# Scores from a high part over a low part, h's place per sublayer, and other distances between softmax stages, in a four-layer trunk

## The chip, the cores and the metric

The kernel runs on one core of one Trainium2 chip. The metric is the device time of one launch in microseconds (us), lower is better. The core has TensorE (PE, matmuls and transposes), VectorE (DVE), ScalarE (ACT), GpSimd (POOL) and SyncE (SP, which issues the loads here); each works through its own list of instructions in order.

## What is computed

Four layers over 512 tokens of width 1024, each a token mixer and a SwiGLU channel mixer (ffn), with a modulation from `c` ahead of each and a layer norm behind it. The change touches the scores of layer 1 (sliding-window attention, swa) and layer 3 (differential attention, diff), h's place in memory in all eight sublayers, and one yield in layer 0 (mLSTM). Cut to these:

```python
for i in range(DEPTH):
    mod = einsum('bd,sde->sbe', silu(c), ada_w[i]) + ada_b[i]          # "ada": 24 columns a sublayer
    h = x * (1 + scale[0]) + shift[0]
    y = (mlstm, swa, hgrn2, diff)[i](h)
    x = layer_norm(alpha * x + (1 + gate[0]) * y)
    h = x * (1 + scale[1]) + shift[1]
    y = swiglu(h, ffn_w_in[i], ffn_w_out[i])
    x = layer_norm(alpha * x + (1 + gate[1]) * y)

# swa: 16 query heads of 64, 2 key heads; 128-query blocks, 256 keys (128 in the first)
s = where(valid, einsum('bqhgd,bkhd->bhgqk', qi, ki) * scale, -inf)
mx = maximum(s.max(-1), sink); p = exp(s - mx); p = p / (p.sum(-1) + exp(sink - mx))

# diff: 8 heads, two score maps each, q and k of 64; 128-query blocks, all keys up to the block's end
p = softmax(where(causal, einsum('bqhcd,bkhcd->bhcqk', qi, k) * scale, -inf))
a = p[:, :, 0] - lam * p[:, :, 1];  out = einsum('bhqk,bkhe->bqhe', a, v)
```

## The kernel before

**Products.** A float32 product is made of fp32r matmuls: `weights` loads a 128 x 1024 tile into one of seven `raw` buffers, ACT rounds it to `wh` (L194), DVE subtracts to get `wl` (L195), and `mm3` issues high x high, high x low and low x high (L204 to L206). h is kept split as well, `hh` and `hl`, one tile each for the whole kernel. The ffn's first half works with seven products of quarters of its operands (`strassen`, L503): some of these take a quarter of h as it is, others a sum of quarters, which is in a tile `tf`. In swa and diff the scores were a single float32 matmul: q of two heads, transposed, lies in the 128 partitions, and the key side `kz` has one head's rows and zeros in the other's, so that one stationary q serves both heads.

**Swa.** A unit is a pair of heads j and a block of 128 queries tb; 8 x 4 units. `unit` is a generator with three stages: scores with mask and maximum (L943, L946 on DVE), exponentials on ACT (L953), DVE's sums, POOL's scaling (L959); then the transposes of the probabilities (L965) and their copy (L967); then the product with v (L974). `pipeline(us, (0, 5, 6))` runs stage 2 five units behind stage 1, and stage 3 six behind. The first half, j = 0 to 3, is merged with the second half's projection of q, which ends with flipping q (transposes, L924); the second half, j = 4 to 7, is merged with half of the output projection. The rotation of q and k (`rope`) is DVE and ACT work on a projection's PSUM bank.

**Diff.** Four groups g of two heads j. A unit is one j and one block tb: two scores of tb + 1 times 128 keys (L1086), mask and maximum (L1088, DVE), exponentials (L1094, ACT), reciprocal and scaling (L1097 and L1098 DVE, L1099 POOL), the combination of both maps (L1100, DVE); then the transposes (L1106) and a copy; then the product with v (L1114); then norm and flip of the output. `flip` (L1038) transposes q or k of one j. `proj(g + 1)`, which makes the next group's q, k and v, is merged with `attend(g)` as fill; for the last group half of the output projection is.

**What sets the order.** `merge` takes in turn the generator that is furthest behind, by the cost that its yields have named against its total. That gives a program order. A scheduler then lists each engine's instructions by its own estimate of when operands and buffers are there; what comes first in the program has priority. PSUM is eight banks of 128 x 512 (`bank()`), taken in turn by all of this; `b4` and `b2` are tiles of pools in SBUF. On the chip each engine keeps its list's order, and PE waits where an operand is late.

**ada.** `weights` also calls `ada_steps`: columns of the next modulations (a load into `raw` and a DVE operation, L128) are spread over the program. `fold` (L341, DVE) adds a finished output tile to the residual.

## Time and profile before

| | us |
|---|---|
| median of 3 runs (2433.79 to 2435.41) | 2435.06 |
| the profiled execution: its own time / its span | 2436.47 / 2434.8 |
| mLSTM, 0 to 238 | 238 |
| swa, 605 to 770 | 165 |
| hgrn, 1135 to 1440 | 305 |
| diff, 1808 to 2058 | 250 |
| the four ffn: from 238, 770, 1440, 2058 | 367, 365, 368, 377 |

In the rows that follow, a group's row gives line, engine, operation, output and inputs, count, then busy time in us, mean ns of one, and the idle time of the engine ahead of them with what ended it. A row of a window gives its length, each engine's busy time with the count of instructions, then the granted TensorE clock (1.00 is full), the share of DMA time and GB/s. A row of the timeline gives start, length and instruction; of the chain that ended last, start, length and line; of the waits, who waited for whom, us in total, times and the longest. A matmul's length runs until its result is there, so matmuls overlap; what one costs is the distance of their starts. A float32 matmul is two records.

### The profile page before, as it was taken

What the parts mean: (1) busy time and instruction counts of PE and PEld (TensorE: products, weight loads), DVE (VectorE), ACT (ScalarE), POOL (GpSimd) and SP (SyncE); (2) the same over time, 40 slices, a digit from 0 to 9 for tenths busy, and PEclk for the clock granted to TensorE, in tenths of its full rate; (3) what the DMA queues carried; (4) which work ended last, traced back from release to release, by engine and by line L of the source; (5) the groups of instructions that cost most, each with busy time, mean ns of one, the idle gap of its engine ahead of it and who ended that gap; (6) DMA issues with size and microseconds to landing.
All of it is one profiled execution on the core that took longest, in us unless ns stands there. A gap on an engine that the chain in (4) does not pass through costs nothing.

```text
span 2434.8 us, 40054 instructions
## 1 busy us (share of the span) xinstructions
PE 2378.1 (98%) x15464; PEld 2123.0 (87%) x15464; DVE 1794.9 (74%) x3137; ACT 1102.6 (45%) x1917; POOL 481.8 (20%) x734
## 2 busy tenths in 40 slices
PE   7999999999899999999999999999999999999998
PEld 5778999998668989899888899898988888999897
DVE  6956988886887978787755569788867556968565
ACT  2534644343553635244333336352445554635343
POOL 5003200004434000006433331000053223100003
PEclk9999999999999999999999999999999999999999
DMA  9832363743411363652521113637525111333331
GB/s 317 285 118 87 105 216 95 245 142 121 144 53 53 103 209 114 232 188 85 162 79 61 35 57 117 205 107 236 186 94 173 62 36 44 109 112 101 106 102 35
DMA packets 93999, 312.31 MB, mean 128 GB/s; under 512 B 10736, under 2 KB 13168, under 8 KB 93808
## 3 DMA queue, kind: packets, MB, share of 16 engines
q1 hardware_dynamic: 92800, 309.43, 39.6%
q8 instruction: 121, 1.98, 0.3%
q14 instruction: 70, 0.57, 0.1%
q10 hardware_dynamic: 1008, 0.32, 0.1%
HBM read 307.62 MB, written 2.10 MB: 127 GB/s over the span
## 4 chain that ended last, share of the span: by engine, by line
PE 80%; DVE 9%; ACT 4%; DMA 3%; POOL 3%; issue 2%; POOLq 0%; ACTq 0%; DVEq 0%; SPq 0%
PE ps L503 27%; PE ps L204 14%; PE ps L206 14%; PE ps L205 14%; DVE wl L195 2%; PE ps L1086 1%; DMA raw<-in_ada_w 1%; PE ps L1252 1%; DVE raw L128 1%; ACT wh L194 1%; PE ps L943 1%; DVE xz L412 1%; POOL H L448 1%; DVE xz L420 1%; DVE hl L449 1%
## 5 line engine op out<-in xcount | busy, mean ns | idle before, releaser
L194 ACT ACTIVATE wh<-raw 128x1024 fp32r<-128x1024 f32 (+1 forms) x251 | 257.9, 1031 | 382.9 <-DMA raw<-in_ffn_out 116.1
L480 ACT ACTIVATE wh<-raw 128x1024 fp32r<-128x1024 f32 x252 | 266.1, 1060 | 351.2 <-PE ps L503 134.2
L503 PE MATMUL ps<-tf,wh 128*128 128x256 f32 x2304 | 410.8, 280 | 0.0
L195 DVE TENSOR_TENSOR wl<-raw,wh 128x1024 fp32r<-128x1024 f32 (+1 forms) x251 | 304.3, 1214 | 99.8 <-ACT wh L194 84.2
L481 DVE TENSOR_TENSOR wl<-raw,wh 128x1024 fp32r<-128x1024 f32 x252 | 305.9, 1221 | 80.1 <-ACT wh L480 78.3
L503 PEld LDWEIGHTS ps<-tf,wh 128*128 128x128 f32 x2304 | 353.3, 188 | 0.9
L503 PE MATMUL ps<-tf,wl 128*128 128x256 f32 x1152 | 321.7, 279 | 0.0
L205 PE MATMUL ps<-pair,wh 128*128 128x512 f32 (+1 forms) x816 | 294.4, 361 | 1.5 <-DVE pair L578 1.3
L204 PE MATMUL ps<-pair,wh 128*128 128x512 f32 (+1 forms) x816 | 294.9, 361 | 0.0
L206 PE MATMUL ps<-pair,wl 128*128 128x512 f32 (+1 forms) x816 | 293.9, 360 | 0.0
L128 DVE CUSTOM_DVE_ANT_0 raw<-raw,cond,adab 128x1024 f32<-128x1024 f32 x192 | 246.6, 1294 | 45.3 <-DMA raw<-in_ada_w 43.9
L341 DVE SCALAR_TENSOR_TENSOR xz<-ps,gate,xz 128x512 f32<-128x512 f32 (+1 forms) x208 | 129.8, 625 | 159.7 <-PE ps L206 159.3
L503 PE MATMUL ps<-hh,wl 128*128 128x256 f32 x864 | 245.0, 284 | 0.0
L503 PE MATMUL ps<-hh,wh 128*128 128x256 f32 x864 | 244.7, 283 | 0.0
L503 PE MATMUL ps<-hl,wh 128*128 128x256 f32 x864 | 244.6, 283 | 0.0
L204 PE MATMUL ps<-wh,hh 128*128 128x512 f32 (+1 forms) x608 | 239.3, 395 | 4.6 <-ACT hh L445 3.3
L204 PE MATMUL ps<-hh,wh 128*128 128x256 f32 (+1 forms) x616 | 208.0, 344 | 18.1 <-ACT wh L194 15.6
L206 PE MATMUL ps<-wh,hl 128*128 128x512 f32 (+1 forms) x608 | 222.5, 366 | 0.0
L205 PE MATMUL ps<-wl,hh 128*128 128x512 f32 (+1 forms) x608 | 222.3, 366 | 0.1
L503 PEld LDWEIGHTS ps<-tf,wl 128*128 128x128 f32 x1152 | 216.7, 188 | 0.0
L206 PE MATMUL ps<-hh,wl 128*128 128x256 f32 (+1 forms) x616 | 209.9, 343 | 5.5 <-DVE wl L195 5.5
L205 PE MATMUL ps<-hl,wh 128*128 128x256 f32 (+1 forms) x616 | 207.9, 340 | 0.2
(292 smaller groups left out, 4957.9 us busy)
## 6 DMA issues: line engine op xcount, KB each, us to landing
raw<-in_ada_w SPq DMA_DIRECT2D x192, 512.0 KB, 4.6
raw<-in_ffn_dp SPq DMA_DIRECT2D x144, 512.0 KB, 3.9
raw<-in_ffn_out SPq DMA_DIRECT2D x64, 448.0 KB, 3.6
raw<-in_ffn_in SPq DMA_DIRECT2D x32, 512.0 KB, 3.7
raw<-in_ffn_out SPq DMA_DIRECT2D x32, 512.0 KB, 4.6
raw<-in_m_vo SPq DMA_DIRECT2D x16, 512.0 KB, 5.8
raw<-in_h_qf SPq DMA_DIRECT2D x16, 512.0 KB, 4.1
raw<-in_h_ig SPq DMA_DIRECT2D x16, 512.0 KB, 3.8
```

The source lines that it names most:

```text
L128: self.nc.vector.tensor_tensor_reduce(w, w, self.cond, 1.0, self.adab[:, sub, j : j + 1], ALU.mult, ALU.add, mod[:, j : j + 1])
L194: nc.scalar.activation(hi[:, :n], raw[:, :n], AF.Copy)
L195: (eng or nc.vector).tensor_tensor(lo[:, :n], raw[:, :n], hi[:, :n].bitcast(F32), ALU.subtract)
L204: nc.tensor.matmul(ps, lhs[0], rhs[0], start=start, stop=False)
L205: nc.tensor.matmul(ps, lhs[0], rhs[1], start=False, stop=False)
L206: nc.tensor.matmul(ps, lhs[1], rhs[0], start=False, stop=stop)
L341: nc.vector.scalar_tensor_tensor(z, ps[:, t], gate[:, d : d + 1], z, ALU.mult, ALU.add)
L412: V.tensor_tensor(z, z, st[:, 0, :], ALU.subtract)
L420: V.tensor_tensor(z, z, st[:, 1, :], ALU.mult)
L480: nc.scalar.activation(hi, raw, AF.Copy)
L481: nc.vector.tensor_tensor(lo, raw, hi.bitcast(F32), ALU.subtract)
L503: nc.tensor.matmul(ps[:, j * 256 : j * 256 + 256], w[a][:, c], m[b], start=first and j == k == a == b == 0, stop=k == 3 and a == 1, skip_g ...
```

## The change

- **h's place.** `hh` and `hl` get tiles that are 128 elements longer. `place(ffn)` lets h begin 16 elements (64 bytes) further in them for an ffn than for a mixer. Pools change places and sizes (`state` behind `sm`; `mod` 24 columns for 32; `lns` 2 for 38), so everything behind them shifts.
- **Scores.** `stacked` makes, for each head of a pair, a tile with the high part of its 64 rows of q in one half of the partitions and their low part in the other. `doubled` makes k's high part, and its low part, in both halves. `mm4` issues q against high and against low: with both halves stacked, two fp32r matmuls give all four partial products. A matmul is at least 256 wide. Zeros and their memsets go. Evictions are now halves of 64 partitions: per pair of heads two on ACT and two on DVE for q, four and four for k.
- **Waiting q and k.** Rotated q (swa) and q and k (diff, in `qkdone` alike) wait in `raw` buffers, two token tiles to a buffer, and not in `b2`. `big` has 13 buffers (12), `mid` 9 (10).
- **Distances.** swa (0, 5, 7) for (0, 5, 6), diff (0, 3, 5, 8) for (0, 3, 4, 6).
- **Diff's flips.** `turn` flips q and k of one j. j = 0's stays in `proj`; j = 1's now opens the group's loop, with three steps of the units after each half, ahead of the merge.
- **mLSTM.** A yield of 2.0 for 0.0 ahead of the transposes of the output, and 11.5 for 9.5 as the total of `mix`.

```diff
-        self.state = pool("state", 1)
         self.adap = pool("adap", 2)
         self.lnp = pool("lnp", 1)
         self.sm = pool("sm", 2)
+        self.state = pool("state", 1)
...
-            self.big, self.mid = pool("big", 12), pool("mid", 10)
+            self.big, self.mid = pool("big", 13), pool("mid", 9)
...
-        self.hh = self.state.tile([P, KD, T], F32R, name="hh")
-        self.hl = self.state.tile([P, KD, T], F32R, name="hl")
+        self.hboth = [self.state.tile([P, KD * T + P], F32R, name=x) for x in ("hh", "hl")]
+        self.place(False)
...
+    def place(self, ffn):
+        o = 16 if ffn else 0
+        self.hh, self.hl = (x[:, o : o + KD * T].rearrange("p (k t) -> p k t", t=T) for x in self.hboth)
...
-        mod = self.adap.tile([P, 32], F32, tag="mod", name=self.nm("mod"), bufs=3)
+        mod = self.adap.tile([P, 24], F32, tag="mod", name=self.nm("mod"), bufs=3)
...
+    def stacked(self, ps):
+        x = self.b4([P, 2, T], F32R)
+        for h in range(2):
+            r, o = slice(64 * h, 64 * h + 64), slice(64 - 64 * h, 128 - 64 * h)
+            self.nc.scalar.activation(x[r, h, :], ps[r, :], AF.Copy)
+            self.nc.vector.tensor_tensor(x[o, h, :], ps[r, :], x[r, h, :].bitcast(F32), ALU.subtract)
+        return x
+    def doubled(self, ps):
+        hi, lo = (self.b4([P, 2, T], F32R) for _ in range(2))
+        for h in range(2):
+            r, o = slice(64 * h, 64 * h + 64), slice(64 - 64 * h, 128 - 64 * h)
+            for x in (r, o):
+                self.nc.scalar.activation(hi[x, h, :], ps[r, :], AF.Copy)
+            for x in (r, o):
+                self.nc.vector.tensor_tensor(lo[x, h, :], ps[r, :], hi[r, h, :].bitcast(F32), ALU.subtract)
+        return hi, lo
+    def in_pairs(self, xs, tt):
+        if tt % 2 == 0:
+            x = self.raw.tile([P, 2, T], F32, tag="raw", name=self.nm("raw"))
+            xs += [x[:, 0, :], x[:, 1, :]]
+        return xs[tt % 2 - 2]
+    def mm4(self, ps, q, ks):
+        for i, k in enumerate(ks):
+            self.nc.tensor.matmul(ps, q, k, start=i == 0, stop=i == 1)
...
-            self.lnp.tile([P, w], F32, tag=x, name=self.nm(x), bufs=2)[:, :2] for x, w in (("lns", 38), ("lnv", 2))
+            self.lnp.tile([P, w], F32, tag=x, name=self.nm(x), bufs=2)[:, :2] for x, w in (("lns", 2), ("lnv", 2))
...
-            yield 0.0
+            yield 2.0
             yield from self.transpose_out(y, 2, acts)
...
-            yield from self.merge((mix(h), 9.5), (fill, 26 if h == H - 2 else 20.8))
+            yield from self.merge((mix(h), 11.5), (fill, 26 if h == H - 2 else 20.8))
...
-            q = self.b2([P, T])
-            self.rope(q, ps, tt, 8)
-            qts.append(q)
+            self.rope(self.in_pairs(qts, tt), ps, tt, 8)
...
-            for jj in range(2):
-                qT = self.b4([P, 2, T])
-                for j in (2 * jj, 2 * jj + 1):
-                    ps = self.bank()
-                    for tt in range(NTT):
-                        nc.tensor.transpose(
-                            ps[:, tt * P : (tt + 1) * P], qt[tt][:, j * P : (j + 1) * P], self.ident
-                        )
-                    nc.scalar.activation(qT[:, j % 2, :], ps, AF.Copy)
-                    qTs.append(qT[:, j % 2, :])
-                    yield 0.5
+            for j in range(4):
+                ps = self.bank()
+                for tt in range(NTT):
+                    nc.tensor.transpose(ps[:, tt * P : (tt + 1) * P], qt[tt][:, j * P : (j + 1) * P], self.ident)
+                qTs.append(self.stacked(ps))
+                yield 0.5
...
-            ps = self.bank()[:, : 2 * nk * P].rearrange("p (h k) -> p h k", h=2)
-            nc.tensor.matmul(ps, qTs[j][:, q], kz[:, :, k0 : k0 + nk * P], start=True, stop=True)
+            ps = self.bank().rearrange("p (h k) -> p h k", h=2)
+            for h in range(2):
+                self.mm4(ps[:, h, :], qTs[j][:, h, q], [x[:, h, k0 : k0 + 2 * P] for x in ks])
...
-            yield from self.pipeline(us, (0, 5, 6))
+            yield from self.pipeline(us, (0, 5, 7))
...
-        for h in range(2):
-            r = slice(64 * h, 64 * h + 64)
-            nc.scalar.activation(kz[r, h, :], ps[r, :], AF.Copy)
+        ks = self.doubled(ps)
...
-            qT = self.b4([P, 2, T])
-            kz = []
-            for j in range(2):
-                if j:
-                    for _ in range(4):
-                        yield next(pv)
-                nc.scalar.activation(qT[:, j, :], flip(qk, j), AF.Copy)
-                z = self.b4([P, 2, T])
-                nc.gpsimd.memset(z[64:, 0, :], 0.0)
-                nc.gpsimd.memset(z[:64, 1, :], 0.0)
-                ps = flip(qk, 2 + j)
-                for m in range(2):
-                    r = slice(64 * m, 64 * m + 64)
-                    nc.scalar.activation(z[r, m, :], ps[r, :], AF.Copy)
-                kz.append(z)
-                yield 1.0
+            yield from turn(g, 0, qk)
             yield from pv
-            res[g] = qT, kz, v
+            res[g] = qk, v
+        def turn(g, j, qk):
+            q = self.stacked(flip(qk, j))
+            yield 0.5
+            res[g, j] = q, self.doubled(flip(qk, 2 + j))
+            yield 0.5
 
         def unit(g, j, tb, hd):
-            qT, kz, v = res[g]
+            qT, ks = res[g, j]
+            v = res[g][1]
             w = (tb + 1) * P
             q = slice(tb * P, w)
             mx, su = (self.small([P, 2], t, bufs=4) for t in ("mx", "su"))
             pr = []
             for m in range(2):
                 ps = self.bank()
-                nc.tensor.matmul(ps[:, :w], qT[:, j, q], kz[j][:, m, :w], start=True, stop=True)
+                n = max(w, 256)
+                self.mm4(ps[:, :n], qT[:, m, q], [x[:, m, :n] for x in ks])
...
-            yield from self.pipeline(us, (0, 3, 4, 6))
+            yield from self.pipeline(us, (0, 3, 5, 8))
 
         yield from proj(0)
         for g in range(4):
             fill = proj(g + 1) if g < 3 else self.out_proj(self.out_srcs(a["d_out"], 0), 2, acts[:4], gate, False)
-            yield from self.merge((attend(g), 17), (fill, 33 if g < 3 else 20.8))
+            units = attend(g)
+            for _ in turn(g, 1, res[g][0]):
+                for _ in range(3):
+                    yield next(units)
+            yield from self.merge((units, 17), (fill, 32 if g < 3 else 20.8))
...
+            self.place(more and plan[i + 1][0] == "ffn")
```

The lines of the changed kernel stand further down: `mm3` is L210 to L212, `mm4` L248, `stacked` subtracts in L226, `doubled` in L236, the flips are L954 (swa) and L1064 (diff), swa's transposes L993, diff's L1124.

**First place: the start of diff's first group, PE.** In the order's rows a name with a number is one tile (`ps_18188` one use of a PSUM bank); `wh_18205,hh` and the like are fill, the next group's projection. Before, from unit 0's scores:

```order
L1086 MATMUL ps_18188<-b_2563_18106,b_2561_18099 128x128
L1086 MATMUL ps_18192<-b_2563_18106,b_2561_18099 128x128
L204 MATMUL ps_18233<-wh_18205,hh 128x512
L205 MATMUL ps_18233<-wl_18206,hh 128x512
L206 MATMUL ps_18233<-wh_18205,hl 128x512
L204 MATMUL ps_18234<-wh_18205,hh 128x512
L205 MATMUL ps_18234<-wl_18206,hh 128x512
L206 MATMUL ps_18234<-wh_18205,hl 128x512
L1086 MATMUL ps_18243<-b_2563_18106,b_2561_18099 128x256
L1086 MATMUL ps_18247<-b_2563_18106,b_2561_18099 128x256
L204 MATMUL ps_18233<-wh_18205,hh 128x512
L205 MATMUL ps_18233<-wl_18206,hh 128x512
```

Now, from the last score of unit 1; `ps_18302` and `ps_18369` hold the flipped q and k of j = 1, and the first L1124 is unit 0's transpose:

```order
L248 MATMUL ps_18338<-b_2563_18238,b_2561_18228 128x256
L248 MATMUL ps_18338<-b_2564_18239,b_2561_18228 128x256
L248 MATMUL ps_18352<-b_2563_18238,b_2561_18228 128x384
L248 MATMUL ps_18352<-b_2564_18239,b_2561_18228 128x384
L248 MATMUL ps_18357<-b_2563_18238,b_2561_18228 128x384
L248 MATMUL ps_18357<-b_2564_18239,b_2561_18228 128x384
L1064 MATMUL ps_18369<-ident,raw_18076 128x128 x2
L1064 MATMUL ps_18369<-ident,raw_18143 128x128 x2
L1124 MATMUL ps_18384<-ident,b_2572_18317 128x128
L248 MATMUL ps_18390<-b_2563_18238,b_2561_18228 128x512
L248 MATMUL ps_18390<-b_2564_18239,b_2561_18228 128x512
L248 MATMUL ps_18395<-b_2563_18238,b_2561_18228 128x512
```

The six fill matmuls between one unit's scores and the next's are gone from here, the flips of j = 1 have come, and unit 0's transpose, which came behind 24 fill matmuls, comes right behind the second flip.

**The same place on DVE.** L1088 is mask and maximum, L1100 the combination that ends a unit's probabilities. Before:

```order
L1088 ISA b_2575_18194,mx_18186<-ps_18192,difmask 128x128
L1088 ISA mx_18186 128x1
L1092 TENSOR_SCALAR mx_18186<-mx_18186 128x2
L195 TENSOR_TENSOR wl_18541<-raw_18538,wh_18540 128x1024
L1097 RECIPROCAL su_18187<-su_18187 128x2
L1088 ISA b_2595_18245,mx_18241<-ps_18243,difmask 128x256
L1088 ISA mx_18241 128x1
L1098 TENSOR_TENSOR su_18187<-su_18187,coef 128x2
L1088 ISA b_2597_18249,mx_18241<-ps_18247,difmask 128x256
L1088 ISA mx_18241 128x1
L1100 SCALAR_TENSOR_TENSOR b_2573_18190<-b_2575_18194,su_18187,b_2573_18190 128x128
L1092 TENSOR_SCALAR mx_18241<-mx_18241 128x2
```

Now (L1106 is mask and maximum, L226 and L236 the low parts of q and k, L1118 the combination of unit 0):

```order
L226 TENSOR_TENSOR b_2568_18307<-ps_18302,b_2568_18307 64x512
L1106 ISA b_2580_18341,mx_18331<-ps_18338,difmask 128x256
L1106 ISA mx_18331 128x1
L1106 ISA b_2584_18355,mx_18350<-ps_18352,difmask 128x384
L1106 ISA mx_18350 128x1
L1115 RECIPROCAL su_18313<-su_18313 128x2
L1110 TENSOR_SCALAR mx_18331<-mx_18331 128x2
L1106 ISA b_2586_18360,mx_18350<-ps_18357,difmask 128x384
L1106 ISA mx_18350 128x1
L1116 TENSOR_TENSOR su_18313<-su_18313,coef 128x2
L236 TENSOR_TENSOR b_2589_18375<-ps_18369,b_2588_18374 64x512
L1118 SCALAR_TENSOR_TENSOR b_2572_18317<-b_2574_18322,su_18313,b_2572_18317 128x128
```

Ahead of unit 0's combination stood one unit's maxima and one weight tile; now stand the maxima of two units more, both low parts of q and one of k's.

**Second place: the middle of swa, PE.** Before, with the scores of units 17 to 19 and unit 16's transposes (L965):

```order
L204 MATMUL ps_6790<-b_1012_6755,wh_6783 128x512
L205 MATMUL ps_6790<-b_1012_6755,wh_6783 128x512
L206 MATMUL ps_6790<-b_1012_6755,wl_6784 128x512
L943 MATMUL ps_6807<-b_829_5848,b_1005_6720 128x512
L943 MATMUL ps_6824<-b_829_5848,b_1005_6720 128x512
L943 MATMUL ps_6841<-b_829_5848,b_1005_6720 128x512
L943 MATMUL ps_6858<-b_829_5848,b_1005_6720 128x256
L965 MATMUL ps_6872<-ident,b_1018_6769 128x128 x2
L943 MATMUL ps_6880<-b_829_5848,b_1005_6720 128x512
```

Now, with unit 16's transposes in L993:

```order
L248 MATMUL ps_6928<-b_861_6132,b_1005_6789 128x256
L211 MATMUL ps_6871<-b_1012_6829,wh_6864 128x512
L212 MATMUL ps_6871<-b_1012_6829,wl_6865 128x512
L248 MATMUL ps_6928<-b_862_6133,b_1005_6789 128x256
L248 MATMUL ps_6948<-b_861_6132,b_1009_6806 128x256
L248 MATMUL ps_6948<-b_862_6133,b_1009_6806 128x256
L248 MATMUL ps_6948<-b_861_6132,b_1009_6806 128x256
L248 MATMUL ps_6948<-b_862_6133,b_1009_6806 128x256
L993 MATMUL ps_6965<-ident,b_1019_6850 128x128 x2
L248 MATMUL ps_6973<-b_861_6132,b_1009_6806 128x256
```

Twelve fill matmuls stood between unit 16's scores (ahead of them) and unit 17's, and the scores were float32; now fp32r scores of five units, with a few fill matmuls among them, are all that lies between.

**The same place on DVE.** Before (L946 is mask and maximum):

```order
L967 COPY b_1009_6742<-ps_6737 128x512
L195 TENSOR_TENSOR wl_7397<-raw_7394,wh_7396 128x1024
L946 ISA b_1018_6769,mx_6764<-ps_6767,swamask,sink 128x128
L946 ISA mx_6764 128x1
L946 ISA b_1018_6769,mx_6764<-ps_6767,swamask,sink 128x128
L946 ISA mx_6764 128x1
L211 TENSOR_TENSOR b_1012_6755<-ps_6681,b_1012_6755 128x512
L949 TENSOR_TENSOR es_6765<-sink,mx_6764 128x2
L950 TENSOR_SCALAR mx_6764<-mx_6764 128x2
```

Now (L974 is mask and maximum, `b_1019_6850` unit 16's tile):

```order
L226 TENSOR_TENSOR b_1005_6789<-ps_6784,b_1005_6789 64x512
L226 TENSOR_TENSOR b_1009_6806<-ps_6801,b_1009_6806 64x512
L226 TENSOR_TENSOR b_1011_6820<-ps_6815,b_1011_6820 64x512
L226 TENSOR_TENSOR b_1005_6789<-ps_6784,b_1005_6789 64x512
L226 TENSOR_TENSOR b_1009_6806<-ps_6801,b_1009_6806 64x512
L226 TENSOR_TENSOR b_1011_6820<-ps_6815,b_1011_6820 64x512
L217 TENSOR_TENSOR b_1012_6829<-ps_6753,b_1012_6829 128x512
L226 TENSOR_TENSOR b_1014_6837<-ps_6832,b_1014_6837 64x512
L974 ISA b_1019_6850,mx_6842<-ps_6845,swamask,sink 128x128
L974 ISA mx_6842 128x1
L974 ISA b_1019_6850,mx_6842<-ps_6845,swamask,sink 128x128
L974 ISA mx_6842 128x1
```

Ahead of unit 16's maxima stood a weight tile; now also stand seven halves of the second half's q.

More of the change, by code (lines that the diff above doesn't have):

```diff
@@ L817, in mlstm @@
             fill = proj(h + 1)
-            yield from self.merge((mix(h), 9.5), (fill, 26 if h == H - 2 else 20.8))
+            yield from self.merge((mix(h), 11.5), (fill, 26 if h == H - 2 else 20.8))
         yield from self.merge(
-            (mix(H - 1), 9.5), (self.out_proj(self.out_srcs(a["m_out"], 0), 2, acts[:4], gate, False), 20.8)
+            (mix(H - 1), 11.5), (self.out_proj(self.out_srcs(a["m_out"], 0), 2, acts[:4], gate, False), 20.8)
         )
@@ L900, in swa @@
         nc.scalar.dma_start(sink, a["s_sink"].partition_broadcast(P))
-        kz = self.b4([P, 2, T])
         gp = nc.gpsimd
-        gp.memset(kz, 0.0)
         kv_ = self.b4([P, 2, NTT, P])
@@ L946, in unit @@
                 nc.vector.tensor_tensor_reduce(
-                    s[:, h, :], ps[:, h, :], ms, 0.125, sk[:, h : h + 1], ALU.add, ALU.max, mx[:, h : h + 1]
+                    s[:, h, :], ps[:, h, : nk * P], ms, 0.125, sk[:, h : h + 1], ALU.add, ALU.max, mx[:, h : h + 1]
                 )
@@ L1043, in qkdone @@
         def qkdone(tt, ps):
-            x = self.b2([P, T])
-            self.rope(x, ps, tt, 8)
-            qks.append(x)
+            self.rope(self.in_pairs(qks, tt), ps, tt, 8)
         def proj(g):
```

## The prediction

> **What bounds the kernel now.** I read the page's engine totals first, then the chain that ended last, then the windows of the stages that the change touches.
>
> ```profile
> PE 2378.1 (98%) x15464; PEld 2123.0 (87%) x15464; DVE 1794.9 (74%) x3137; ACT 1102.6 (45%) x1917; POOL 481.8 (20%) x734
> PE 80%; DVE 9%; ACT 4%; DMA 3%; POOL 3%; issue 2%; POOLq 0%; ACTq 0%; DVEq 0%; SPq 0%
> 605.00:770.00 165.00, 157.99 (x969) 117.99 (x968) 128.00 (x446) 85.31 (x240) 67.66 (x127) 1.00 0.25 82
> 647.00:751.00 104.00, 101.99 (x595) 68.58 (x593) 82.85 (x335) 54.91 (x185) 37.55 (x79) 1.00 0.15 48
> 770.00:1135.00 365.00, 361.74 (x2527) 337.50 (x2526) 302.06 (x419) 169.59 (x222) 51.27 (x85) 1.00 0.48 154
> 1808.00:2058.00 250.00, 245.21 (x1459) 208.09 (x1459) 156.03 (x480) 135.14 (x346) 69.60 (x124) 1.00 0.26 83
> 1843.00:2040.00 197.00, 194.55 (x1123) 163.04 (x1122) 117.03 (x390) 106.24 (x297) 42.59 (x81) 1.00 0.23 73
> ```
>
> TensorE is busy 98% of the span. The windows are the swa layer and its attention part, one ffn, the diff layer and its attention part (columns: length, then PE, weight loads, DVE, ACT, POOL). Even in attention PE stands still for only 2.0 us (104.00 − 101.99) in swa and 2.5 us in diff. So a matmul made shorter is worth its time, if its operands come as early as PE then wants them; DVE has room on average (20% free in swa's attention, 40% in diff's), which says nothing of single places. The profiled execution took 2436.47 us, 1.7 more than its span and 1.4 more than the median of the runs, 2435.06; I sum against 2436.5 and take 1.4 off at the end. A measurement of this kernel can tell about 0.2% (4.9 us) from no change.
>
> **Scores as two fp32r products.** One f32 score matmul is two records in the trace.
>
> ```profile
> L943 PE MATMUL ps<-b,b x64: 377/592/602, 647.2 to 738.4; 128*128 128x512 f32 x48, 128*128 128x256 f32 x16
> 640.07 0.12 PE ps L205
> 650.32 0.23 PE ps L206
> 650.55 0.88 PE ps L943 x2
> L1086 PE MATMUL ps<-b,b x128: 270/434/595, 1843.7 to 2027.8; 128*128 128x128 f32 x32, 128*128 128x256 f32 x32, 128*128 128x384 f32 x32, 128*128 128x512 f32 x32
> 1843.69 0.61 PE L1086 MATMUL ps<-b,b 128*128 128x128 f32 x4
> 1845.52 1.03 PE L1086 MATMUL ps<-b,b 128*128 128x256 f32 x4
> 1847.77 0.81 PE L1086 MATMUL ps<-b,b 128*128 128x384 f32 x2
> ```
>
> In the chain of waits each piece is the time from one matmul to the next: 0.12 us for a 256-wide fp32r matmul, 0.23 for a 512-wide one, 0.88 for a 512-wide f32 score (both records). In swa 24 such scores and 8 of half the width cost 24 × 0.87 + 8 × 0.43 = 24.3 us; after, every unit has four 256-wide fp32r matmuls, 32 × 4 × 0.12 = 15.4 us: **−8.9 us**. In diff a record takes (0.61 − 0.27)/3 = 0.11 us at 128 (0.27 is the least duration of that line), about 0.22, 0.32 and 0.43 at the other widths, so the four units of one j, two maps of two records each, cost 4 × 1.08 = 4.3 us. After: widths 256, 256, 384, 512, two maps of two products, 4 × (0.12 + 0.12 + 0.17 + 0.23) = 2.6 us (0.17 interpolated). 1.75 us × 8 = **−14 us**. This presumes that PE finds its operands, which is the question of the next two parts.
>
> **The wait at each start of a diff group.** Before, unit 0's scores went in between fill matmuls, and its transposes came long after its softmax.
>
> ```profile
> 1844.56 0.29 DVE L1088 CUSTOM_DVE_ANT_0 b<-ps,difmask 128x128 f32<-128x128 f32 x1
> 1844.77 0.28 DVE L1088 CUSTOM_DVE_ANT_0 b<-ps,difmask 128x128 f32<-128x128 f32 x1
> 1847.53 0.35 DVE L1100 SCALAR_TENSOR_TENSOR b<-b,su,b 128x128 f32<-128x128 f32 x1 [0.24 <-POOL b L1099]
> 1851.83 0.27 PE L1106 MATMUL ps<-ident,b 128*128 128x128 f32 x1
> L1088 DVE CUSTOM_DVE_ANT_0 b<-ps,difmask 128x384 f32<-128x384 f32 x16 | 8.5, 550 | 1.3 <-PE ps L1086 1.3
> 667.89 0.60 DVE b L211
> ```
>
> Scores start at 1843.69, the probabilities are ready at 1847.88 (1847.53 + 0.35), the transpose runs at 1851.83: 4 us of cover. The order of the changed kernel has taken that cover away. With j = 1's `turn` at the group's start, PE does four transposes of q, twelve score matmuls of units 0 to 2, four transposes of k, and then wants unit 0's transpose; six score banks and two flip banks are all eight of PSUM, so no fill can stand there. That is 8 × 0.11 + 4 × (0.12 + 0.12 + 0.17) = 2.5 us of PE work. Unit 0's first score is out after about 0.9 us (0.45 of transposes, two products, 0.2 until the result is there). From then DVE has, in its order, two mask-and-max of 128 (0.21 each by their starts), two q subtractions (0.60 each, the L211 row; 64 rows of 512 are not in this trace, and I take the same), two of 256 (0.34), two of 384 (0.48), five small operations (0.1), one k subtraction (0.60), and unit 0's combine (0.35): 4.7 us. The transpose can start at 0.9 + 4.7 = 5.6, PE is there at 2.5: **a wait of 3.1 us**. Unit 1's transposes wait about 0.3 us more (a subtraction, three small ones and a 0.40 combine, 1.3 us, against four 512-wide products, 0.9), and the second halves of k some 0.5 us. Some 4 us a group, four groups: **+16 us** (from 0, if DVE works through its queue sooner than this count has it, to 22, if ACT's exponentials and POOL's step come on top of it). Diff's scores thus net +2 us, between −14 and +8.
>
> **The wait in the middle of swa.** After four heads' pairs the second half of q is flipped.
>
> ```profile
> 697.24 1.36 PE L924 MATMUL ps<-ident,b 128*128 128x128 f32 x11
> 705.47 0.38 PE L965 MATMUL ps<-ident,b 128*128 128x128 f32 x2
> 697.44 0.69 DVE L967 COPY b<-ps 128x512 f32<-128x512 f32 x1 [0.45 <-PE ps L965]
> 698.05 1.22 DVE L195 TENSOR_TENSOR wl<-raw,wh 128x1024 fp32r<-128x1024 f32 x1
> 702.84 0.73 DVE L341 SCALAR_TENSOR_TENSOR xz<-ps,gate,xz 128x512 f32<-128x512 f32 x1
> 703.12 0.72 POOL L959 TENSOR_SCALAR b<-b,su 128x128 f32<-128x128 f32 x2 [5.59 <-DVE su L957]
> L128 DVE CUSTOM_DVE_ANT_0 raw<-raw,cond,adab 128x1024 f32<-128x1024 f32 x192 | 246.6, 1294 | 45.3 <-DMA raw<-in_ada_w 43.9
> ```
>
> Before, PE reached unit 16's transposes at 705.47, and POOL had its probabilities by 703.84. After, PE's way from the flips to them is some 7.5 us (704.7 on this scale), since the scores are shorter. DVE, free of the weight subtraction at 699.3, has seven halves of `stacked` and the low part of an activation, 8 × 0.60, then the two mask-and-max, 0.6, to 704.7; then an ada column of 1.29, another half, 0.60, and the fold of 0.73 before it negates the maximum, 707.4; then come two exponentials on ACT (about 0.9), DVE's sum and reciprocal behind four mask-and-max of the next units, and POOL's 0.72: about 709.9. **A wait of 5 us** (0 if the ada column's data come late and the rest slips in, 6 if ACT's half copies are in the way too). At swa's start k's four doubled low halves, 4 × 0.60, stand before the first maxima and I add 1.2 us (half of them hidden by five units' scores). Swa: −8.9 + 5 + 1.2 = about −2.7; DVE has 12 us more to do there (16 + 4 subtractions of 0.60) on 82.85 of 104, so **−2 us**, ends −9 and +3.
>
> **h 64 bytes further in the ffn.** By the pools' sizes in the code, h and the weight tiles start before at the same offset modulo 512 bytes, and tf (sums of h's quarters) 64 bytes beyond that; after, h in an ffn is 64 beyond too.
>
> ```profile
> L503 PE MATMUL ps<-tf,wh 128*128 128x256 f32 x2304 | 410.8, 280 | 0.0
> L503 PE MATMUL ps<-hh,wh 128*128 128x256 f32 x864 | 244.7, 283 | 0.0
> 439.80 0.40 PE L503 MATMUL ps<-tf,wh 128*128 128x256 f32 x2
> 442.27 0.29 PE L503 MATMUL ps<-hh,wh 128*128 128x256 f32 x1
> 442.40 0.28 PE L503 MATMUL ps<-hl,wh 128*128 128x256 f32 x1
> 446.00 0.28 PE L503 MATMUL ps<-hl,wh 128*128 128x256 f32 x1
> ```
>
> 21 matmuls with tf lie between 439.80 and 442.27, 117.6 ns each; 30 with h between 442.40 and 446.00, 120.0 ns each. If the offset is the cause, 3 × 864 matmuls gain 2.4 ns: **−6 us**. That the two tiles' places differ is all that the trace shows; the whole memory also shifts by 32 bytes modulo 64, so 0 and +6 are the other ends. I take −6, since the one pair of rows that tells places apart says it.
>
> The Trainium skill, page "SBUF — State Buffer", section "Who interferes with whom", speaks against this term: moving operand and weights have read ports of their own, and "PE and ACT never wait on anyone". By it the place is worth nothing; the rows of 117.6 and 120.0 ns differ without a wait, and do not agree with it as it stands.
>
> **Waits that go, and the clock.**
>
> ```profile
> PE ps L677 <- DVE b L1123: 2.3, 4, 0.6
> PE ps L677 <- DVE b L801: 1.8, 2, 1.2
> PE ps L1252 <- POOL b L1292: 2.3, 1, 2.3
> 1176.70:1180.10 3.40, 3.40 (x13) 2.92 (x12) 1.42 (x3) 1.32 (x4) 1.44 (x4) 0.50 0.46 171
> ```
>
> mLSTM's transposes waited 1.8 us for DVE; the new yield puts fill ahead: **−1.5**. In diff the wider skew should end the 2.3 us before L677: **−2**. The wait of 2.3 us for POOL (at 1173.1) was followed by 3.4 us at a granted clock of 0.50, which is 1.7 us lost. The changed kernel gets up to five such lulls (four group starts, swa's middle), so 0 to +8.5; I take half, **+4**. The Trainium skill, page "TensorE: Matmul & The Clock Gate", section "What's actually happening", lets the clock fall only after an idle window of about 3.4 us; by it waits of 3.1 us would mostly be spared and the sum be lower by some 3; the 2.3 us row shows that a shorter lull can do it.
>
> Costed at nothing: the memsets that go (POOL is 20% busy); rotated q in `raw` buffers, which takes two of seven from weights in flight (DMA is at 0.25 of its time in swa and diff; with no cover, one weight's landing late per layer, some 3 us); ACT's added half copies (85 of 165 us and 135 of 250 us busy); hgrn, whose order does not change.
>
> **Sum.** −2 (swa) + 2 (diff) − 6 (place) − 3.5 (old waits) + 4 (clock) = −5.5 us: 2431.0 against 2436.5, and 1.4 off for the median: **2429.5**.
>
> **Rivals.**
> - *The waits are covered* (chance 0.25). For it: DVE has 40% free in diff's attention, and my queue at the group's start is one hand count. Against it: the order leaves PE nothing else to do there. Then diff gives −14, swa −7, no clock loss: −14 − 7 − 6 − 3.5 = −30.5, that is 2404.6.
> - *The group starts cost more than the scores save* (0.18; slower). The same wait, with what stands ahead of unit 0's maxima on DVE counted in: a weight subtraction of 1.22 and an ada column of 1.29, and each lull followed by the half clock, 1.7. A start then costs 3.1 + 1.22 + 1.29 + 1.7 = 7.3 us, four cost 29.2: 29.2 − 14 − 2 − 6 − 3.5 + 2 (clock in swa) = +5.7, that is 2440.8. It decides from about 5.9 us a start, where the other terms (14 + 2 + 6 + 3.5 − 2) are used up.
> - *h's place changes nothing* (0.17): the two rows differ for another reason, such as tf's being written by other engines. Then −5.5 + 6 = +0.5: 2435.6. This is also the case in which that part of the change doesn't do what it says.
>
> **How the numbers follow.** Forecast 0.40 (2424 to 2435). Of it 0.24 lies below 2430.2, 0.15 within 0.2%, 0.01 above 2439.9; with the covered case faster is 0.49. The place case gives 0.09 to no change and, with its own waits larger, 0.08 to slower; same 0.24, slower 0.18 + 0.08 + 0.01 = 0.27. The range 2405 to 2442 takes in the covered and the slower case about their middles, leaving out near 0.2.
>
> **What would show it.** PE waits of about 3 us for DVE in front of unit 0's transpose (L1124) four times in diff, and of about 5 us at L993 once in swa; 117.6 ns between ffn matmuls on h; granted clock 0.5 behind these lulls; L801 gone from PE's waits. The forecast is wrong if those waits are under 1 us (then near 2405), or if h's matmuls stay at 120 ns.

## The result and the profile after

The changed kernel takes 2467.72 us (median of 4 runs, 2465.91 to 2470.34) against 2435.20 before (4 runs): a ratio of 1.0134, interval 1.0122 to 1.0147. Forecast were 2429.5 and a range of 2405 to 2442. It is slower, by 32.5 us.

The page of the changed kernel, engine totals and the chain that ended last:

```profile
PE 2369.6 (96%) x15528; PEld 2131.5 (87%) x15528; DVE 1837.5 (75%) x3205; ACT 1125.6 (46%) x1951; POOL 468.2 (19%) x717
PE 80%; DVE 8%; ACT 4%; POOL 3%; DMA 2%; issue 2%; POOLq 0%; ACTq 0%; DVEq 0%; SPq 0%
L539 PE MATMUL ps<-hh,wh 128*128 128x256 f32 x864 | 241.5, 280 | 0.0
```

PE is busy for 8.5 us less than before (2378.1), and the span is 28.9 us longer. The third row is the ffn's matmul on h, 280 ns where it was 283; the starts of 46 of these between 300.61 and 305.91 are 117.8 ns apart, where the prediction had read 120.0 before. To see where the time is, both kernels are cut at the first and last `strassen` matmul of each ffn (L503, now L539). First before, then after; the windows are the first ffn, swa with what lies around it, and diff with what lies around it:

```profile
284.40:551.07 266.67, 266.67 (x1897) 251.60 (x1895) 222.89 (x259) 118.56 (x144) 1.48 (x5) 1.00 0.54 171
551.07:816.07 265.00, 254.66 (x1596) 204.60 (x1594) 206.88 (x606) 136.38 (x318) 109.08 (x173) 1.00 0.28 91
1755.37:2106.97 351.60, 344.27 (x2104) 298.07 (x2102) 235.49 (x636) 187.69 (x425) 111.82 (x170) 1.00 0.28 90
```

```profile
280.82:545.75 264.93, 264.93 (x1896) 249.85 (x1895) 222.50 (x259) 118.48 (x144) 1.09 (x5) 1.00 0.53 172
545.75:821.07 275.32, 253.73 (x1659) 215.28 (x1658) 217.87 (x626) 142.46 (x328) 104.36 (x172) 0.96 0.27 88
1754.74:2137.90 383.16, 347.67 (x2103) 305.31 (x2102) 269.35 (x684) 204.53 (x449) 101.37 (x154) 0.95 0.26 83
```

An ffn is 1.7 us shorter (four of them: 7 us), the stage up to the first ffn 3.6 us (280.82 for 284.40), swa 10.3 us longer and diff 31.6. In swa PE now stands still for 21.6 us (length less PE busy; 10.3 before), in diff for 35.5 (7.3), and the mean granted clock is 0.96 and 0.95. The stretches at 0.50 add up to 23.9 us in swa and 37.6 in diff; half of what PE was busy in them, taken here as the time that the slow clock cost, is 8.4 and 15.7 us (0 and 1.7 before). Over the whole kernel, by the same sum: 37.5 us more of standing still, 19.7 more lost to the half clock, and, as what is left of the change in PE's busy time, 28.2 less work. Together this is the 28.9 us, up to rounding.

Who PE waited for after, in total over the span:

```profile
PE ps L210 <- ACT wh L200: 35.0, 12, 13.8
PE ps L1124 <- DVE mx L1110: 13.6, 4, 4.4
PE ps L993 <- POOL b L987: 5.4, 1, 5.4
PE ps L1124 <- DVE b L1118: 3.8, 3, 1.3
PE ps L713 <- DVE b L1141: 2.8, 4, 0.9
PE ps L248 <- ACT b L234: 2.4, 3, 1.1
PE ps L1064 <- POOL raw L914: 1.8, 3, 0.8
```

The waits at L1124 (17.4 us), L993 (5.4) and L248 (2.4) are those that the prediction had worked out. (What unit 0's transpose needs is the combination L1118; the row names the small operation L1110, which DVE ends last ahead of the transpose.) The first row is not among them: PE's wait for the rounded weights was 16.8 us before. Where the rest comes from shows at the start of swa, in SP's waits, SP's own timeline (issues of loads) and PE's:

```profile
SPq L133 <- PE ps L954: 16.4, 1, 16.4
620.25 0.33 SPq L133 DMA_DIRECT2D raw<-in_ada_w  x1
621.92 0.33 SPq L197 DMA_DIRECT2D raw<-in_s_q  x1
626.56 1.22 PE L210 MATMUL ps<-wh,hh 128*128 128x256 f32 x4 [4.73 <-ACT wh L200]
```

SP issues loads in order. An ada column's turn came for a `raw` buffer that held rotated q, and SP stood for 16.4 us until the flips (L954) had read it. The weight tile behind it went out at 621.92, and PE, which wanted it, stood for 4.7 us. At swa's end the same queue is late again:

```profile
SPq L133 <- PE ps L954: 67.0, 2, 50.6
SPq L197 <- DVE mod L134: 17.7, 3, 15.6
747.68 6.38 SPq L197 DMA_DIRECT2D raw<-in_s_out  x4
752.46 0.58 PE L210 MATMUL ps<-b,wh 128*128 128x256 f32 x1 [6.50 <-ACT wh L200]
```

The first row, of all of swa, has a second such stand, of 50.6 us, until the second half's flips had read their q. Seven ada columns went out only behind it, from 692.53 on, and the four loads of the output projection's second half then waited for the buffers of these columns, which DVE was late to use (second row). Before, these four loads went out between 678 and 700.

### The profile page after: what moved, and what is told of

Its sections match the earlier page's. It is cut to its first block, busy times and chain, and to the rows that moved or that the text cites. A ratio compares the mean times of both kernels' runs of the same rounds, so it can differ in the third digit from the quotient of the medians.

```text
span 2463.7 us, 40253 instructions
## 1 busy us (share of the span) xinstructions
PE 2369.6 (96%) x15528; PEld 2131.5 (87%) x15528; DVE 1837.5 (75%) x3205; ACT 1125.6 (46%) x1951; POOL 468.2 (19%) x717
## 4 chain that ended last, share of the span: by engine, by line
PE 80%; DVE 8%; ACT 4%; POOL 3%; DMA 2%; issue 2%; POOLq 0%; ACTq 0%; DVEq 0%; SPq 0%
PE ps L539 27%; PE ps L212 14%; PE ps L211 14%; PE ps L210 14%; DVE wl L201 2%; PE ps L1274 1%; PE ps L248 1%; DMA raw<-in_ada_w 1%; ACT wh L200 1%; DVE raw L134 1%; POOL H L484 1%; DVE xz L448 1%; PE ps L1335 1%; DVE xz L456 1%; PE ps L821 1%
## 5 line engine op out<-in xcount | busy, mean ns | idle before, releaser
L539 PE MATMUL ps<-tf,wh 128*128 128x256 f32 x2304 | 410.1, 279 | 0.0
L539 PEld LDWEIGHTS ps<-tf,wh 128*128 128x128 f32 x2304 | 352.5, 187 | 1.0
L539 PE MATMUL ps<-tf,wl 128*128 128x256 f32 x1152 | 321.5, 279 | 0.0
L211 PE MATMUL ps<-pair,wh 128*128 128x512 f32 (+1 forms) x816 | 294.3, 361 | 1.3 <-DVE pair L614 1.3
L210 PE MATMUL ps<-pair,wh 128*128 128x512 f32 (+1 forms) x816 | 294.8, 361 | 0.0
L212 PE MATMUL ps<-pair,wl 128*128 128x512 f32 (+1 forms) x816 | 293.8, 360 | 0.0
L210 PE MATMUL ps<-wh,hh 128*128 128x512 f32 (+1 forms) x608 | 232.1, 386 | 12.5 <-ACT wh L200 12.5
L539 PE MATMUL ps<-hh,wh 128*128 128x256 f32 x864 | 241.5, 280 | 0.0
L539 PE MATMUL ps<-hl,wh 128*128 128x256 f32 x864 | 241.1, 279 | 0.0
L539 PE MATMUL ps<-hh,wl 128*128 128x256 f32 x864 | 241.1, 279 | 0.0
L210 PE MATMUL ps<-hh,wh 128*128 128x256 f32 (+1 forms) x616 | 207.6, 343 | 18.8 <-ACT wh L200 16.0
L211 PE MATMUL ps<-wl,hh 128*128 128x512 f32 (+1 forms) x608 | 223.9, 369 | 1.1 <-DVE wl L201 1.0
L212 PE MATMUL ps<-wh,hl 128*128 128x512 f32 (+1 forms) x608 | 223.9, 369 | 0.0
L539 PEld LDWEIGHTS ps<-tf,wl 128*128 128x128 f32 x1152 | 216.4, 188 | 0.0
L212 PE MATMUL ps<-hh,wl 128*128 128x256 f32 (+1 forms) x616 | 209.6, 342 | 4.9 <-DVE wl L201 4.9
L211 PE MATMUL ps<-hl,wh 128*128 128x256 f32 (+1 forms) x616 | 207.5, 339 | 0.1
```

The source lines that it names most:

```text
L210: nc.tensor.matmul(ps, lhs[0], rhs[0], start=start, stop=False)
L211: nc.tensor.matmul(ps, lhs[0], rhs[1], start=False, stop=False)
L212: nc.tensor.matmul(ps, lhs[1], rhs[0], start=False, stop=stop)
L539: nc.tensor.matmul(ps[:, j * 256 : j * 256 + 256], w[a][:, c], m[b], start=first and j == k == a == b == 0, stop=k == 3 and a == 1, skip_g ...
```

## The experiments

Each starts from the kernel named; times are medians, with the kernel before run on the same chip (2435.1 to 2436.1).

**Rotated tiles in b2 again** (from the changed kernel).

```diff
-            self.rope(self.in_pairs(qts, tt), ps, tt, 8)
+            q = self.b2([P, T])
+            self.rope(q, ps, tt, 8)
+            qts.append(q)
```

and the same in `qkdone`.

> The changed kernel, with rotated q (swa) and q and k (diff) waiting in b2 buffers as before, and all seven raw buffers left to loads; the diff flips, distances and pool sizes stay as changed. Theory A (rotated tiles hold raw buffers, so weights land late): the waits of PE for the high parts of weights fall from 35.0 us to near the 16.8 us of before, and the two half-clock stretches behind those in swa go (each 6.8 us, 3.4 us lost): about 2467.7 - 18 - 7 = 2443 us. Theory B (only the group starts of diff and DVE's extra work matter, and the late weights come from that): the weight waits stay above 30 us and the time within 4 us of 2467.7.

2449.05 us (ratio 1.0058, interval 1.0043 to 1.0073). Its row of PE's waits for weights, and its windows of swa and diff, cut as above:

```profile
PE ps L210 <- ACT wh L200: 16.8, 6, 13.4
545.36:806.51 261.15, 247.73 (x1660) 209.99 (x1659) 216.29 (x626) 141.68 (x328) 108.31 (x172) 0.99 0.28 93
1740.29:2118.52 378.23, 346.51 (x2103) 303.60 (x2102) 269.50 (x684) 203.34 (x449) 103.67 (x154) 0.95 0.26 84
```

The wait is back at the 16.8 us of before. Swa is 14.2 us shorter than in the changed kernel and 3.9 shorter than before; the clock there is 0.99. Diff gains 4.9. Theory A: the weight waits go, and of swa's half clock 1.7 us are left of 8.4, which is the 25 us that it gave. The time is still 6 us above its 2443, since other waits of PE come up: in swa those beside the one for weights and unit 16's are 8.5 us by their rows, where they were 3.9. Diff's half clock stays at 15.0 us for 15.7.

**Flips of j = 1 in the projection again** (from the changed kernel).

```diff
             yield from turn(g, 0, qk)
+            for _ in range(4):
+                yield next(pv)
+            yield from turn(g, 1, qk)
             yield from pv
...
-            units = attend(g)
-            for _ in turn(g, 1, res[g][0]):
-                for _ in range(3):
-                    yield next(units)
-            yield from self.merge((units, 17), (fill, 32 if g < 3 else 20.8))
+            yield from self.merge((attend(g), 17), (fill, 33 if g < 3 else 20.8))
```

> The changed kernel, with the flips of j = 1 of a diff group back in the projection (behind four more of its steps, as before) and no steps of the units ahead of the merge. Theory A (flips at the group's start take PE's cover): the 17.4 us of waits at the probabilities' transposes go to under 3, the half-clock stretches behind them (four of them, 3.4 to 6.8 us each) too, diff is shorter by about 17 + 10 = 27 us: 2441 us. Theory B (DVE is too slow with the halves of q and k wherever they stand): the waits move to other places, diff is shorter by less than 10 us: above 2458.

2449.62 us (1.0061, 1.0046 to 1.0076). Its window of diff and its largest waits:

```profile
1757.93:2123.69 365.76, 337.24 (x2104) 299.00 (x2103) 268.00 (x684) 201.18 (x449) 100.88 (x154) 0.98 0.27 87
PE ps L210 <- ACT wh L200: 34.1, 12, 13.6
PE ps L211 <- DVE wl L201: 9.2, 5, 2.8
```

Diff is 17.4 us shorter and its clock 0.98 for 0.95; the waits at the probabilities' transposes in diff are 4.9 us for 17.4. But the expected 27 us don't come, and the time lies between the two theories': the waits for the high parts of weights stay (second row, 35.0 in the changed kernel), and those for low parts grow (third row, 1.0 there); in diff PE waits three times 1.4 us for the one and 2.7 for the other.

**Both.**

> Both edits, rotated tiles in b2 and the flips of j = 1 in the projection. If the two causes are apart and add up: about 2467.7 - 25 - 27 = 2416 us. If they are one cause seen twice (late loads make the group starts late): no better than the better of the two alone, about 2441. The wait of 5.4 us in swa's middle stays in both.

2421.25 us (0.9946, 0.9931 to 0.9960), 46.5 us under the changed kernel where the two alone give 18.7 and 18.1, and 5 us above the 2416 given for the sum. The wait in swa's middle stays, at 4.3 us.

```profile
545.53:808.22 262.69, 249.08 (x1660) 210.54 (x1658) 216.61 (x626) 141.79 (x328) 108.37 (x172) 0.99 0.28 93
1742.93:2093.78 350.85, 330.86 (x2103) 293.21 (x2102) 267.77 (x684) 201.62 (x449) 109.75 (x154) 1.00 0.28 91
```

The causes are two, and in diff each hides part of the other: 383.2 us with both, 378.2 or 365.8 with one undone, 350.9 with both undone. There is no half clock left in diff. Yet diff is only 0.7 us shorter than before, at 13.4 us less PE busy time: PE stands still there for 20.0 us, 12.7 more than before, most of it in eleven waits of 0.8 to 1.5 us at the transposes and products of the attention units.

**Place and mLSTM alone** (from the kernel before: `place`, the pools' order and sizes but for `big` and `mid`, and the two numbers of mLSTM; no line of swa or diff).

> The kernel before, with only h's place (pools in the changed order and sizes, h 64 bytes further for an ffn) and the mLSTM yields of the change; scores, flips and waiting tiles as before. The stage accounting of the changed kernel gives 1.7 us less in each of four ffn and 3.6 us less in mLSTM: 2435.2 - 7.0 - 3.6 = about 2424.6. If mLSTM's gain came from a chance of its waits only, 2426 to 2428; if h's place works only together with the other tiles' sizes, 2431 to 2435.

2427.23 us (0.9966, 0.9954 to 0.9979). The ffn are at 264.6 to 265.5, the first stage at 280.5 for 284.4. The time lies where a lost gain in mLSTM had been put, but that gain is there; what is missing is that diff is 2.5 us and swa 1.1 us longer than before without a change in their code. So of the 14.4 us by which the kernel with both edits beats the one before, place and mLSTM have 8.4, and the some 20 us of PE work that the scores save bring 6.

**h not shifted** (from the kernel with both).

```diff
-        o = 16 if ffn else 0
+        o = 0
```

> The faster of the kernels so far (rotated tiles in b2, flips in the projection, 2421 us), with h at the same place for ffn and mixers (offset 0), pools as changed. Theory A (the 64 bytes between h and the weights make the gain): each ffn is back at 266.7 us from 264.9, the time at 2421.3 + 7 = 2428. Theory B (the shift of all tiles by the pools' new order makes it): no difference, 2421.

2427.78 us (0.9965, 0.9952 to 0.9978). Its windows of the first two ffn, and the other two are alike:

```profile
280.53:547.20 266.67, 266.67 (x1897) 251.58 (x1895) 223.15 (x259) 118.43 (x144) 1.57 (x5) 1.00 0.53 171
809.53:1076.20 266.67, 266.67 (x1897) 251.58 (x1895) 223.57 (x259) 118.70 (x144) 1.55 (x5) 1.00 0.53 171
```

Theory A to 0.5 us: the 64 bytes make the 1.7 us an ffn, not the pools' order. Why they do is not shown.

**PE kept busy in the wait at a group's start** (from the changed kernel).

```diff
+            if j:
+                for _ in range(26):
+                    nc.tensor.transpose(res["spare"][:, T - P :], self.ident, self.ident)
...
+                if j == 0 and tb == 2:
+                    res["spare"] = ps
```

> The changed kernel, with 26 transposes of the identity into an unread part of a score bank, in PE's order right behind the second flip of each diff group, where PE waited 3.1 to 4.4 us for unit 0's probabilities. They take about 26 x 0.11 = 2.9 us, so PE works through the wait and the wait's end stays where DVE sets it; DVE's order is the same. Theory A (the half clock behind each of these waits is a cost of its own): the stretches at 0.50 behind the four waits go (3.4 + 3 x 6.8 us, half of it lost), and the time falls by 8 to 11 us to about 2458, though PE has more to do. Theory B (PE waits for DVE there anyway, the slower clock only uses up slack): within 3 us of 2467.7, or above by the added work.

2469.94 us (1.0145, 1.0127 to 1.0162). It doesn't tell the theories apart, since the added transposes waited themselves (their line is L1094 here):

```profile
PE ps L1094 <- DVE mx L1112: 10.8, 4, 3.3
```

They write to a bank that DVE still read from, so they ran behind the wait and not in it. The price of the slow clock was measured in another way:

**Lulls of set length** (behind the last layer of the kernel with both).

```diff
+        for n in ns:
+            ps = self.bank()
+            nc.tensor.transpose(ps[:, :P], x[:, :P], self.ident)
+            for i in range(45):
+                nc.tensor.matmul(ps, self.hh[:, i % KD, :P], self.hh[:, i % KD, :], start=i == 0, stop=i == 44)
+            x = self.b2([P, T])
+            for _ in range(n):
+                nc.scalar.activation(x, ps, AF.Copy)
```

> The faster kernel with an addition behind its last layer: 18 bursts of 45 matmuls of 512 wide (10 us each), and ahead of each burst but the first a lull in which PE waits for a chain of 1 to 9 copies by ACT (about 0.5 us each), so lulls of about 0.8 to 5 us, each length twice. Theory A (a lull of some 2.3 us or more puts the clock to 0.50 for 3.4 or 6.8 us behind it, one of 1.7 us or less does not): half-clock stretches from the fourth length up, none below the third, and a burst behind one takes 1.7 to 3.4 us longer. Theory B (what sets it is not the lull but the mix of work ahead of it): stretches do not follow the lull's length. The time itself, some 2421 + 230 us, says nothing.

From its one execution, 2694.32 us, PE's timeline: each transpose with the lull ahead of it in brackets, and the burst of 45 matmuls behind it with its length; then the clock in two windows:

```profile
2443.07 0.33 PE L1431 MATMUL ps<-ident,b 128*128 128x128 f32 x1 [1.37 <-ACT b L1436]
2443.16 10.49 PE L1433 MATMUL ps<-hh 128*128 128x512 f32 x45
2455.60 0.33 PE L1431 MATMUL ps<-ident,b 128*128 128x128 f32 x1 [1.95 <-ACT b L1436]
2455.68 12.08 PE L1433 MATMUL ps<-hh 128*128 128x512 f32 x45
2470.33 0.33 PE L1431 MATMUL ps<-ident,b 128*128 128x128 f32 x1 [2.58 <-ACT b L1436]
2470.42 10.48 PE L1433 MATMUL ps<-hh 128*128 128x512 f32 x45
2484.10 0.48 PE L1431 MATMUL ps<-ident,b 128*128 128x128 f32 x1 [3.21 <-ACT b L1436]
2484.23 13.19 PE L1433 MATMUL ps<-hh 128*128 128x512 f32 x45
2455.88:2459.29 3.41, 3.41 (x10) 2.63 (x9) 0.00 (x0) 0.00 (x0) 0.00 (x0) 0.50 0.00 0
2483.19:2490.01 6.82, 5.91 (x15) 4.66 (x16) 0.00 (x0) 0.83 (x2) 0.00 (x0) 0.50 0.00 1
```

A lull of 1.37 us costs nothing behind it; of 1.95, 1.6 us (12.08 for 10.49), of 3.21, 2.7 us. But the one of 2.58 us is free, in both passes. Theory A's limit is wrong in that point. All stretches of the half clock begin a multiple of 3.41 us apart (2455.88 and 2483.19 are eight times 3.41 apart). On that grid the lull of 1.95 us lies wholly in one window, and the one of 2.58 is cut into 1.77 and 0.80: what seems to count is the idle time within a window, with the limit between 1.77 and 1.95 us. That reading fits these lulls.

Other traces test it, since the grid falls at another place of the program in each execution. This kernel and the one with both edits are the same up to the end of the last layer, and in both PE waits 1.67 us at the same matmul of diff (starts 1807.36 and 1808.22). Windows along the grid, first of this run, then of the kernel with both:

```profile
1803.94:1807.35 3.41, 1.45 (x8) 0.74 (x6) 2.30 (x7) 1.80 (x3) 1.02 (x2) 1.00 0.75 274
1807.35:1810.76 3.41, 3.40 (x8) 2.72 (x9) 3.25 (x8) 3.22 (x6) 1.96 (x4) 0.50 0.04 14
1803.47:1806.88 3.41, 2.78 (x14) 1.72 (x12) 1.97 (x7) 0.90 (x2) 0.71 (x1) 1.00 0.92 326
1806.88:1810.29 3.41, 2.07 (x9) 1.53 (x9) 3.31 (x9) 2.80 (x5) 1.90 (x3) 1.00 0.31 112
1810.29:1813.71 3.42, 3.42 (x16) 2.46 (x14) 3.35 (x11) 3.42 (x7) 1.65 (x3) 1.00 0.00 0
```

Here the wait and a shorter one lie in one window, which is idle for 1.96 us, and a window of half clock follows; there the grid cuts them into 0.63 and 1.34 us, and none follows. In all fourteen traces, past their first 41 us, windows at full clock that were idle for up to 1.67 us kept it, and the 61 that were idle for 1.90 us or more lost it; in between eight kept it and eight lost it. Apart from these stand 27 windows with four to eight of the layer norm's matmuls of one column: they lost it with 0.58 to 1.65 us idle by the records. A window at half clock with 0.59 us idle or more was always followed by another. That is why a lull of 3.2 us, which runs on into the slow window (0.91 us of it), brings 6.8 us and not 3.4.

**Other distances, and late or early flips** (all from the kernel with both): both old distances; only diff's old; one q flip of swa's second half ahead of its units and three as fill; a diff group's last transposes put off into the next group, with the new and with diff's old distances.

> The same faster kernel with the old distances, (0, 5, 6) in swa and (0, 3, 4, 6) in diff. If the wider distances are what covers the longer softmax chain: waits at the transposes of the probabilities and at the products with v come up, 2426 to 2432. If the waits left in diff (four of 1.5 us at the output's transposes, which the wider distance puts to the group's end) are made by them: 2416 to 2419.

> The faster kernel (rotated tiles in b2, flips in the projection, 2421 us) with diff's old distances (0, 3, 4, 6), swa's new ones kept. In the run with both old distances diff was 1.4 us shorter and swa 1.5 us longer, 3.7 us of it half clock. If both were made by the distances: 2419 to 2420. If swa's half-clock stretch came by the phase of the clock's windows, which any shift of the program moves: anywhere from 2419 to 2424, with swa again changed though its code is the same.

2421.95 us (0.9941, 0.9926 to 0.9956) and 2420.44 (0.9939, 0.9926 to 0.9953): no difference to 2421.25 that these runs can tell, and the first is in neither of the two ranges given for it. Diff is 1.3 us shorter in both, swa 1.5 longer, also where its code is the same.

> The same faster kernel, with only one of the second half's four q flips in swa ahead of the second half's units, and the other three as fill among them; so DVE has two halves of q ahead of unit 16's maxima and not seven. If the queue on DVE makes the wait of 4.3 us at unit 16's transposes: that wait falls under 1 us, a half-clock stretch behind it goes, swa is 4 to 6 us shorter, 2416. If PE's order simply lacks fill there: the wait stays above 3 us, 2420 to 2424.

2424.63 us, as neither theory had it: the wait at unit 16 falls from 4.3 to 2.0 us, but PE now waits 2.3 us at a flip ahead of it and 1.4 at a score, and swa is 3.8 us longer. Its half clock there is 6.8 us behind the flip and 3.4 behind unit 16's wait, where the kernel with both has 6.8 in all.

> The faster kernel (rotated tiles in b2, flips in the projection, 2421 us), with the last stage of a diff group's last unit (the transposes of the normed output) put off into the next group's units. If the four waits of 1.5 us at these transposes are only the end of a group with nothing behind them: three of them go, 2416 to 2418. If PE meets the same wait a little later: within 1.5 us of 2421.

> The same with the old distances (0, 3, 4, 6) in diff, which were 1.4 us better in the diff stage by themselves. If both gains add: 1 to 2 us under the run with (0, 3, 5, 8), 2415 to 2417; if the shorter distance needs the last stage at the group's end: 2419 to 2422.

2423.17 us (0.9954, 0.9937 to 0.9971) and 2424.75 (0.9958, 0.9943 to 0.9973): neither gains, and both are above the ranges given. The wait has moved, here in the first of the two:

```profile
PE ps L1131 <- DVE mx L1117: 6.7, 4, 2.4
PE ps L713 <- DVE b L1148: 3.3, 2, 3.0
```

L713's waits were 4.7 us, L1131's for the same DVE line 4.1. In the second run PE waits 6.4 us, in nine pieces, at the products with v. So the kernel with both edits stays the fastest, with either distances.

## Why the prediction was wrong

- **Scores and h's place** held in the main: −8.9, −14 and −6 were forecast, and PE's work, without the half clock's share, fell by 9.3 us in swa, 10.6 in diff and 7 in the ffn. That the whole, 28.2, comes so near to 28.9 is partly luck, since diff's scores gave a quarter less and other stages a little. The run without the shift shows that the place is the cause in the ffn.
- **The waits at the group starts and in swa's middle** held: 16 and 5 us were forecast, and 17.4 + 2.4 and 5.4 came; for the 1.2 us at swa's start no row of PE's waits stands. The one at a group's start was 3.1 forecast and 3.1 three times (4.4 the first time, where a weight's subtraction stood ahead of unit 0's maxima on DVE). The price taken for a half of 64 partitions on DVE held too; its row after, with the 687 ns that L211 had for all 128:

```profile
L226 DVE TENSOR_TENSOR b<-ps,b 64x512 fp32r<-64x512 f32 x32 | 21.4, 687 | 4.5 <-ACT b L225 3.6
```

- **"Costed at nothing: rotated q in `raw` buffers"** is the step that failed. The prediction looked at how busy the DMA engines are (0.25), gave some 3 us with no cover and put nothing into the sum. The runs show 18.7 us for the edit alone, and 28.4 where the flips stand in the projection (2449.6 to 2421.3). It was not the transfer that was short of time, but the buffer: what stays in it until a flip stops the whole in-order queue of SP behind it, and with it weights for another stage.
- **The clock's term** was mis-sized: +4 was taken, from one stretch of 3.4 us at half the clock behind a 2.3 us wait and half of five such; 19.7 us more than before is what the accounting has. Swa and diff have eleven such stretches and not five (weight waits bring some, the layer norm behind swa one), and seven of them are of 6.8 us: a lull of 3.2 us is followed by that, and in the lull run its price is 2.7 us, where 1.7 was used. The clock cost at most what the accounting says, since a slow stretch takes nothing where PE would have waited: the kernel with both edits and both old distances has 3.4 us of half clock in its first stage, and that stage takes 280.69 us against 280.60 without.
- **Old waits**: mLSTM's 1.8 us went (that stage is 3.6 us shorter, −1.5 forecast; a half clock stretch of 3.4 us went from it too, which the grid gives or takes). Diff's did not: 2.3 us at L677 are 2.8 at L713.

The named slower rival, four group starts of 7.3 us, 29.2 together, has its place right, and its price too: 19.8 us of waits and 9.7 of half clock, and with the rotated tiles in `b2` the flips' place is worth 27.8 (2449.05 to 2421.25). Its make-up is not right, and that the price matches is luck: a weight and an ada column kept DVE from unit 0's maxima in the first group alone, and by the accounting the clock took 2.4 us a start, not 1.7. It alone would have ended at 2440.8; the rest is the buffer with the clock behind it. Weights (18.2 us) and clock (15.7) are 33.9 of the 34.5 us between the −5.5 forecast and the +29.0 of the accounting; the other terms' misses are smaller and of both signs.

## What to carry to other kernels

A tile that waits in a load buffer is paid for by the loads behind it: ask when it will be read, and what the loading engine's queue holds then, not how busy the transfer engines are. Work put ahead of a loop's fill takes the cover from the first dependent step of that loop, and cheaper matmuls make that cover shorter still: some 20 us of PE work saved were worth 6. Count a PE wait of 2 us or more with what the clock does behind it; in which runs one of 1.7 us costs as much is up to the grid.

## What was not expected of the hardware

The half clock follows a grid of 3.41 us, and 1.9 us of idle time within one window of it are enough: lulls of 1.95 us brought 3.4 us of half clock, lulls of 3.2 to 5.1 us 6.8 us, and a lull of 2.58 us, cut by the grid, none. The Trainium skill ("TensorE: Matmul & The Clock Gate", "What's actually happening") has a free-running window of about 3.4 us, which the grid agrees with, and lets the clock fall after an idle window; in these traces the window need not be idle throughout. An h that starts 64 bytes further makes an ffn 1.7 us shorter (264.93 for 266.67 us), though PE stands still in neither; that h and the weights else start at the same offset modulo 512 bytes is read from the pools' sizes in the code, and no other distance was run.
